# Diagonal masks on VectorE, and the weight sums and low parts made ahead on GpSimd's queue, in a hybrid decoder layer

## The chip, the cores and the metric

The kernel runs on one core of one Trainium2 chip. The metric is the device time of one execution in microseconds (us). An engine's instructions run in the order of its own queue; between engines only semaphores order the work. PE is TensorE, ACT is ScalarE, DVE is VectorE, POOL is GpSimd, SP is SyncE, which here only issues DMAs.

## The reference

One layer over 512 tokens of width 1024, batch 1:

```python
h = rms_norm(x, g_mix)
qa, ka, va, qb, kb, vb, gates = split(h @ w_in)            # 8 + 8 heads of 64
ya = moba_attention(rope(qa), rope(ka), va)                # causal softmax, blocks of 256
yb = stick_breaking_attention(qb, kb, vb)
#   z = q.k / 8; causal where s < t (strictly); log_1m = where(causal, -softplus(z), 0)
#   after = reverse exclusive cumsum(log_1m); a = where(causal, exp(log_sigmoid(z) + after), 0); y = a @ v
g = sigmoid(gates + b_gate)
x = x + (g[0] * (ya @ w_a) + g[1] * (yb @ w_b)) @ w_out
h = rms_norm(x, g_ffn)
u = causal_depthwise_conv(h @ w_up, conv_w, conv_b)        # width 3
x = x + (silu(u_gate) * u_val) @ w_down                    # d_ff 2816
out = rms_norm(x, g_final)
```

## The kernel before

All products are in float32 precision made of three fp32r matmuls: a weight block `raw` [128 x 1024] is loaded, ACT copies it to `whi` (the high part), DVE subtracts to get `wlo` (the low part), and `mm3` (L75) multiplies high by high, high by low, low by high: L76, L77, L78. `wload` (L59) does load and split; `raw` has five buffers, `whi`/`wlo` three, so the split of a weight waits until PE has finished the weight three places earlier.

The order of PE's instructions is the order in which the code is written. Of the other engines' instructions a scheduler sets the order from estimated times; where `issue_after` or the helper `inline` (L709) is used, the order on ACT and DVE is written out by hand.

The stages, with their times in the profile:

- 0 to 33 us: norm and the first projections. 33 to 131: attention a (two calls of `attend`, L426), with other projections as fillers between its steps (the lists GAPS).
- 131 to 222: attention b, the stick-breaking one, two calls of `attend` for two head pairs each. A call has three units of query tiles: unit 0 holds tiles 0 and 1, unit 1 tile 2, unit 2 tile 3. For each unit and pair, `weights_b` (L397) takes the scores from PSUM: ACT writes s1 = sigmoid(-z) and be = sigmoid(z), POOL masks the diagonal 128-column blocks of both for both heads (`affine_select`, L406: above the diagonal s1 becomes 1 and be 0), DVE runs a reversed product scan of s1 into R (L414) and multiplies be by it (L416). Then `turn` transposes the result on PE (L443, tile `tp`, one buffer) and ACT copies it out (L446, tile `aT`). s1 (named `a1`), be (`a2`) and R have two buffers each. The filler projections end in DVE instructions that empty a PSUM bank of `pmm` (two buffers): `o` (L338, L340) for q and k, `g` (L489) for the gates.
- 222 to about 340 us, the gates stage: the loop over `KT` (L567): gate projections (`g`), branch products with the weights `ab`, and `split_ahead` twice in an iteration.
- about 340 to 390: the out projection (weights `out`, sums `osum`), the residual x1 and its norm (`x1_add`, `x1_sq`, `x1_scale`), transposes (`x1_turn`) and their drains `x1_out`, which write the high and low rows `h` that the up projection multiplies. This passage is called the up seam.
- 390 to 610: the up projection with convolution and gate. Row tiles 4 to 15 (`MIXED`) are multiplied in a Winograd-like scheme of 7 products for 8 that needs sums of weight blocks, `usum`. 610 to 728: the down projection, final norm and output.

The sums: `sums_of` (L238) makes `usum` of one row tile by four DMAs on POOL's queue, DRAM to DRAM: a copy of 1024 KB, an accumulating add of 512 KB, two accumulating adds of 256 KB. Six tiles are made from 30 us on, with the four `osum` of the out projection; the other six are queued behind the last `affine_select` of attention b. `split_ahead` makes the low part of usum blocks 2 and 3 for nine of the tiles ahead of time: a load `praw` on SP's queue, the high part `phi` on ACT (L562), the difference on DVE (L564), a store to DRAM, `ulo`, on SP's queue. In the mixed stage `wmix` (L889) then loads `wlo` from `ulo` on POOL's queue (L896) for these tiles, and computes it on DVE (L899) for the other three.

Of the kernel before, what the change touches and what calls it, by code (L numbers as in the profile page):

```python
# [10 lines left out]
F32 = mybir.dt.float32  # L11
F32R = mybir.dt.float32r
BF = mybir.dt.bfloat16
AF = mybir.ActivationFunctionType
OP = mybir.AluOpType
# [11 lines left out]
NWARM = 9 * (448,) + (128,)  # L27
NP = FT // 2
MIXED = range(4, 16)
EARLY = 6  # L30
AHEAD = MIXED[:9]
NL = 3
WORDER = ([(n, k) for n in ("qk0", "va") for k in range(4)] + [("vb", g, h) for g in range(2) for h in range(2)]
          + [("mqk", n, i) for n in range(2) for i in range(2)] + [("sqk", p, n) for p in range(4) for n in range(2)]
# [8 lines left out]
def trunk_layer(ctx: ExitStack, tc: tile.TileContext, x: bass.AP, xT: bass.AP, w: bass.AP, vec: bass.AP,  # L43
                gfin: bass.AP, trig: bass.AP, out: bass.AP):
    nc = tc.nc

    def pool(stack, name, bufs, space=None, side=None):
        kw = {}
        if space is not None:
            kw["space"] = space  # L50
        if side is not None:
            kw["side"] = side
        return stack.enter_context(tc.tile_pool(name=name, bufs=bufs, reuse_waits="tile", **kw))

    ctx.enter_context(tc.manual_schedule(engines={mybir.EngineType.PE}))
    consts = pool(ctx, "consts", 1)
    wraw = pool(ctx, "wraw", 5)
    wsp = pool(ctx, "wsp", 3)
# [78 lines left out]
    xp = pool(st1, "xp", 6)  # L137
# [6 lines left out]
    for n in NWARM:  # L144
# [3 lines left out]
    nc.gpsimd.affine_select(out=mf, in_=mf, pattern=[[-1, 128]], compare_op=OP.is_ge, fill=NEG, base=0,  # L148
                            channel_multiplier=1)
    nc.vector.tensor_copy(maskb, mf)  # L150
    xks = {}

    def square(k):
# [65 lines left out]
    def flat(key, n):  # L219
        return w[WIDX[key]:WIDX[key] + n].rearrange("i p (h c) -> (i p h c)", h=2).rearrange("(n p c) -> n p c", p=128, c=512)  # L220

    def adds(out, in_):
        nc.gpsimd.dma_start(out, in_, accum_op=OP.add, max_dma_last_dim=8192)
# [3 lines left out]
    with tc.issue_after(nc.gpsimd.tensor_copy(small[:, 31:], r1[:, :1]).ins):  # L227
        for j, q in enumerate(osum):
            nc.gpsimd.dma_start(q, flat(("oi", j, 0), 2), max_dma_last_dim=8192)
        for j, q in enumerate(osum):  # L230
            adds(q[0:2], flat(("oi", j, 2), 1))
        for q in osum:
            adds(q[2], q[1])
        for q in osum:
            adds(q[3], q[2])
        usum = {i: wdr.tile([4, 128, 512], F32, name=f"usum{i}") for i in MIXED}

        def sums_of(pairs, n=3):  # L238
            for group in (pairs[j:j + n] for j in range(0, len(pairs), n)):
                for i in group:  # L240
                    nc.gpsimd.dma_start(usum[i], flat(("ui", i, 0), 2), max_dma_last_dim=8192)
                for i in group:
                    adds(usum[i][0:2], flat(("ui", i, 2), 1))
                for i in group:
                    adds(usum[i][3], usum[i][0])
                for i in group:
                    adds(usum[i][2], usum[i][3])

        sums_of(MIXED[:EARLY])

    mqkp = pool(ysta, "mqkp", 4, side="right")
    hlp = pool(ysta, "hlp", 2, side="right")
# [36 lines left out]
    def fill(n):  # L289
        while n > 0 and fillers:  # L290
            try:
                n -= next(fillers[0])
            except StopIteration:
                fillers.pop(0)
# [97 lines left out]
                nc.vector.tensor_scalar(a[:, h, o:o + n], a[:, h, o:o + n], st_[:, 1, i:i + 1], None, op0=OP.mult)  # L392
        return a

    selects = []

    def weights_b(sc, seg):  # L397
        W = seg[-1][1] + seg[-1][2]
        s1 = att.tile([128, 2, 512], F32, name="a1")
        nc.scalar.activation(s1[:, :, :W], sc[:, :, :W], AF.Sigmoid, scale=-1.0)  # L400
        be = att.tile([128, 2, 512], F32, name="a2")
        nc.scalar.activation(be[:, :, :W], sc[:, :, :W], AF.Sigmoid)
        for z, fill in ((s1, 1.0), (be, 0.0)):
            for qt, o, n in seg:
                zz = z[:, :, o + n - 128:o + n]
                selects.append(nc.gpsimd.affine_select(out=zz, in_=zz, pattern=[[0, 2], [-1, 128]],  # L406
                                                       compare_op=OP.is_ge, fill=fill, base=-1, channel_multiplier=1))
        R = att.tile([128, 2, 514], F32, name="R", bufs=2)
        for j, (qt, o, n) in enumerate(seg):
            r0 = o + j  # L410
            nc.vector.memset(R[:, :, r0 + n:r0 + n + 1], 1.0)
            for h in range(2):
                z = s1[:, h, o:o + n]
                nc.vector.tensor_tensor_scan(R[:, h, r0:r0 + n][:, ::-1], z[:, ::-1], z, 1.0,  # L414
                                             op0=OP.mult, op1=OP.bypass)
            nc.vector.tensor_mul(be[:, :, o:o + n], be[:, :, o:o + n], R[:, :, r0 + 1:r0 + n + 1])  # L416
        return be
# [90 lines left out]
    gsig = pool(ysta, "gsig", 6, side="right")  # L508
    attend("b", (0, 1), GAPS_B)
    attend("b", (2, 3), GAPS_B)  # L510
    with tc.issue_after(selects[-1].ins):
        sums_of(MIXED[EARLY:])
    fill(1000)
    psA.close()
    psB = ExitStack()
# [32 lines left out]
    psp = pool(tst, "psp", 1)  # L548
    ulo = {i: wdr.tile([128, 2, 512], F32R, name=f"ulo{i}") for i in AHEAD}
    ahead = list(AHEAD)  # L550

    def both(q):
        return q.rearrange("h p c -> p h c")

    def split_ahead():
        if not ahead:
            return
        i = ahead.pop(0)
        raw = psp.tile([128, 2, 512], F32, name="praw", bufs=2)
        nc.sync.dma_start(raw, both(usum[i][2:4]))  # L560
        hi = psp.tile([128, 2, 512], F32R, name="phi")
        nc.scalar.activation(hi, raw, AF.Copy)  # L562
        lo = raw.bitcast(F32R)
        nc.vector.tensor_sub(lo, raw, hi.bitcast(F32))  # L564
        nc.sync.dma_start(ulo[i].bitcast(F32), raw)

    for i in range(KT):  # L567
        if i >= NG:
# [32 lines left out]
    osp = pool(ost, "osp", 4, side="right")  # L601
# [92 lines left out]
    def x1_add(t, h):  # L694
        sl = slice(h * 512, (h + 1) * 512)
        op = nc.vector.tensor_sub if h else nc.vector.tensor_add
        ins = op(x1[:, t, sl], x1[:, t, sl], oq[f"c{t // 2 + 1}{h + 1}"][t % 2])
        nc.sync.dma_start(x1D[t][:, sl], x1[:, t, sl])
        return ins
# [4 lines left out]
    def x1_sq(t, h):  # L704
        return nc.scalar.activation(sqj, x1[:, t, h * 512:(h + 1) * 512], AF.Square, accum_out=sums2[:, h, t:t + 1])
# [3 lines left out]
    def inline(*steps):  # L709
        for f in steps:  # L710
            n = len(nc.cur_bb.bb.instructions)
            with ExitStack() as st:
                for i in tail.values():
                    st.enter_context(tc.issue_after(i))
                f()
            for i in nc.cur_bb.bb.instructions[n:]:
                if i.engine in (mybir.EngineType.DVE, mybir.EngineType.Activation):
                    tail[i.engine] = i

    def x1_scale(T):  # L720
        ts = slice(2 * T, 2 * T + 2)
        v, *rest = (small[:, 8 * T + 2 * i:8 * T + 2 * i + 2] for i in range(4))
        nc.vector.tensor_add(v, sums2[:, 0, ts], sums2[:, 1, ts])
        nc.vector.tensor_scalar(v, v, 1.0 / D, EPS, op0=OP.mult, op1=OP.add)
        r = rsqrt(v, *rest)
        for h in range(2):
            sl = slice(h * 512, (h + 1) * 512)
            for t in range(2):
                o, i, c = x1n[T][:, t, sl], x1[:, 2 * T + t, sl], r[:, t:t + 1]
                if t:  # L730
                    nc.scalar.activation(o, i, AF.Copy, scale=c)
                else:
                    nc.vector.tensor_scalar(o, i, c, None, op0=OP.mult)
# [9 lines left out]
    def x1_out(T, h, order=(0, 2, 1, 3)):  # L743
        for i in order:
            k = 4 * h + i
            src = turn_banks[T, h][i // 2][:, (i % 2) * 256:(i % 2 + 1) * 256]
            hl = h2[k][:, :, T * 256:(T + 1) * 256]
            act = nc.scalar.activation(hl[:, 0], src, AF.Copy, scale=gffn[:, k:k + 1])  # L748
            dve = nc.vector.scalar_tensor_tensor(hl[:, 1], src, gffn[:, k:k + 1], hl[:, 0].bitcast(F32),  # L749
                                                 op0=OP.mult, op1=OP.subtract)  # L750
# [4 lines left out]
    def upload_hi(p):  # L755
        raw = rload(("up",) + upq.pop(0))
        wup.append((p.tile([128, 1024], F32R, name="whi"), p.tile([128, 1024], F32R, name="wlo"), raw))
        nc.scalar.activation(wup[-1][0], raw, AF.Copy)

    def upload_lo(n):  # L760
        hi, lo, raw = wup[n]
        nc.vector.tensor_sub(lo, raw, hi.bitcast(F32))
# [14 lines left out]
           *(lambda t=t: x1_add(t, 1) for t in (2, 3)), lambda: upload_hi(wsp), lambda: upload_hi(wsp))  # L777
    inline(lambda: nc.scalar.activation(sqj[:, :1], padt[:, :1], AF.Sqrt), *(lambda t=t: x1_sq(t, 1) for t in (2, 3)))
    inline(*(lambda t=t, f=f: f(t, 0) for t in (2, 3) for f in (x1_add, x1_sq)), lambda: upload_lo(0))
    inline(lambda: x1_scale(1), lambda: upload_lo(1), *(lambda t=t, f=f: f(t, 0) for t in range(2) for f in (x1_add, x1_sq)))  # L780
    for t in range(2):
        for j, (xs, wa) in enumerate(second):
            mm3(oq["c12"][t], tuple(xs[:, c, 1, t * 128:(t + 1) * 128] for c in range(2)), blk(wa, 1, 512),
                False, j == HP - 1, skip_group_check=True)
            if t == 1 and j == 1:
                for h in range(2):
                    x1_turn(1, h)
    inline(lambda: x1_add(0, 1), lambda: x1_out(1, 0), lambda: x1_out(1, 1), lambda: x1_sq(0, 1), lambda: x1_add(1, 1),
           lambda: upload_hi(osp), lambda: x1_sq(1, 1), lambda: upload_lo(2), lambda: x1_scale(0), lambda: upload_hi(wsp))
    UPB = (6, 7, 4, 5, 0, 1, 2, 3)  # L790
    upn = [0]

# [367 lines left out]
```

## Time and profile before

| what | value |
|---|---|
| median of 3 runs | 727.8 us (727.79 to 728.9) |
| the profiled execution | 729.69 us, span 728.0 us |
| busy in the span: PE, DVE, ACT, POOL | 710.0, 560.7, 389.6, 85.9 us |
| granted TensorE clock, mean of the span | 0.990 |
| DMA share: SP's queue (q1), POOL's queue (q0) | 41.0%, 22.4% of 16 engines |

The span is the time from the first to the last instruction. Rows of the timeline begin with the start in us from the span's start and the duration in us; the bracket at a row's end is the time that the engine sat idle before it, and what ended that. Rows of waits give total us, times, longest us.

### The profile page before, as it was taken

The numbers are of one execution on the slowest core, as the hardware profiler recorded it, in microseconds if no ns is written. First come the engines' busy times: TensorE is split into PE (matmuls) and PEld (weight loads), VectorE is DVE, ScalarE is ACT, GpSimd is POOL, SyncE is SP. The second block draws the span as 40 slices with busy tenths as digits, with TensorE's granted clock in tenths as the row PEclk, the third lists the DMA queues.
The fourth block names the chain that finished last, engine by engine and source line by source line (L and its number), as shares of the span: only waits on it lengthen the run. The fifth ranks groups of instructions, "written<-read, shape, count | busy, mean of one in ns | idle before, by whom it ended". The sixth has DMA issues, their size and how long they took to land.

```text
span 728.0 us, 11232 instructions
## 1 busy us (share of the span) xinstructions
PE 710.0 (98%) x4316; PEld 612.7 (84%) x4316; DVE 560.7 (77%) x830; ACT 389.6 (54%) x582; POOL 85.9 (12%) x130
## 2 busy tenths in 40 slices
PE   9999999999999995999999999999999999999996
PEld 6888888889888884878879899999998888888884
DVE  7678867593973715577786898888999878988987
ACT  6335534563653304346375656766666445455764
POOL 0212333230432230000003300000000000000000
PEclk9999999999999997999999999999999999999998
DMA  8799999121149998757756937776655322567703
GB/s 313 265 341 327 249 235 243 57 88 59 62 141 362 255 259 302 268 199 251 271 173 211 225 93 240 233 259 209 212 184 164 113 91 87 171 197 249 266 13 117
DMA packets 45830, 146.60 MB, mean 201 GB/s; under 512 B 5072, under 2 KB 5840, under 8 KB 41680
## 3 DMA queue, kind: packets, MB, share of 16 engines
q1 hardware_dynamic: 37280, 103.08, 41.0%
q0 software_dynamic: 8208, 42.47, 22.4%
q8 instruction: 34, 0.56, 0.3%
q10 hardware_dynamic: 288, 0.33, 0.1%
q14 instruction: 20, 0.16, 0.1%
HBM read 132.75 MB, written 42.47 MB: 241 GB/s over the span
## 4 chain that ended last, share of the span: by engine, by line
PE 75%; DMA 12%; issue 4%; DVE 4%; ACT 3%; POOL 0%; SPq 0%; POOLq 0%; ACTq 0%; DVEq 0%
PE b L77 10%; PE b L78 10%; PE b L76 10%; PE mm L76 7%; PE mm L78 6%; PE mm L77 6%; DMA praw<-usum 5%; PE c L76 4%; PE c L78 4%; PE c L77 4%; PE q L188 3%; DMA usum<-w 3%; PE tp L443 2%; DMA usum<-usum 2%; PE tp L465 2%
## 5 line engine op out<-in xcount | busy, mean ns | idle before, releaser
L77 PE MATMUL b<-h,whi 128*128 128x256 f32 (+1 forms) x336 | 109.2, 325 | 0.2
L76 PE MATMUL b<-h,whi 128*128 128x256 f32 (+1 forms) x336 | 108.8, 324 | 0.5 <-ACT h L748 0.5
L78 PE MATMUL b<-h,wlo 128*128 128x256 f32 (+1 forms) x336 | 108.6, 323 | 0.0
L71 ACT ACTIVATE whi<-raw 128x1024 fp32r<-128x1024 f32 (+2 forms) x70 | 68.4, 985 | 72.2 <-PE b L77 22.5
L72 DVE TENSOR_TENSOR wlo<-raw,whi 128x1024 fp32r<-128x1024 f32 (+2 forms) x70 | 78.7, 1132 | 20.2 <-ACT whi L71 19.9
L76 PE MATMUL mm<-xg,whi 128*128 128x512 f32 x224 | 89.9, 401 | 0.0
L78 PE MATMUL mm<-xg,wlo 128*128 128x512 f32 x224 | 87.4, 390 | 0.0
L77 PE MATMUL mm<-xg,whi 128*128 128x512 f32 x224 | 87.3, 390 | 0.0
L76 PEld LDWEIGHTS b<-h,whi 128*128 128x128 f32 x336 | 63.9, 190 | 5.9 <-ACT h L748 0.9
L77 PEld LDWEIGHTS b<-h,whi 128*128 128x128 f32 x336 | 63.9, 190 | 5.8 <-DVE h L749 0.8
L78 PEld LDWEIGHTS b<-h,wlo 128*128 128x128 f32 x336 | 63.9, 190 | 4.9
L619 ACT ACTIVATE whi<-raw 128x1024 fp32r<-128x1024 f32 x45 | 46.8, 1051 | 35.4 <-DVE raw L637 16.2
L897 ACT ACTIVATE whi<-raw 128x1024 fp32r<-128x1024 f32 (+1 forms) x48 | 45.6, 951 | 34.6 <-PE b L77 28.9
L619 DVE TENSOR_TENSOR wlo<-raw,whi 128x1024 fp32r<-128x1024 f32 x45 | 54.7, 1221 | 7.4 <-ACT whi L619 7.2
L78 PE MATMUL b<-xa,wlo 128*128 128x256 f32 x192 | 54.5, 284 | 1.1 <-DMA wlo<-ulo 1.1
L76 PE MATMUL b<-xa,whi 128*128 128x256 f32 x192 | 54.3, 283 | 0.0
L77 PE MATMUL b<-xa,whi 128*128 128x256 f32 x192 | 54.3, 283 | 0.0
L76 PEld LDWEIGHTS mm<-xg,whi 128*128 128x128 f32 x224 | 42.1, 188 | 10.2 <-issue 1.8
L78 PEld LDWEIGHTS mm<-xg,wlo 128*128 128x128 f32 x224 | 42.1, 188 | 9.1
L77 PEld LDWEIGHTS mm<-xg,whi 128*128 128x128 f32 x224 | 42.2, 188 | 7.8
L899 DVE TENSOR_TENSOR wlo<-raw,whi 128x1024 fp32r<-128x1024 f32 (+1 forms) x39 | 41.3, 1058 | 9.4 <-ACT whi L897 8.9
L78 PEld LDWEIGHTS b<-xa,wlo 128*128 128x128 f32 x192 | 36.8, 192 | 1.5 <-DMA wlo<-ulo 1.5
(260 smaller groups left out, 1641.4 us busy)
## 6 DMA issues: line engine op xcount, KB each, us to landing
raw<-w SPq DMA_DIRECT2D x113, 512.0 KB, 4.2
usum<-w POOLq DMA_DIRECT2D x12, 1024.0 KB, 22.9
raw<-usum SPq DMA_DIRECT2D x24, 512.0 KB, 4.2
usum<-w POOLq DMA_DIRECT2D x12, 512.0 KB, 20.8
usum<-usum POOLq DMA_DIRECT2D x24, 256.0 KB, 11.1
raw<-w SPq DMA_DIRECT2D x22, 256.0 KB, 5.0
praw<-usum SPq DMA_DIRECT2D x9, 512.0 KB, 6.3
ulo<-praw SPq DMA_DIRECT2D x9, 512.0 KB, 3.8
```

The lines of the kernel that those rows point to most:

```text
L71: nc.scalar.activation(hi[:, sl], raw[:, sl], AF.Copy)
L72: nc.vector.tensor_sub(lo[:, sl], raw[:, sl], hi[:, sl].bitcast(F32))
L76: nc.tensor.matmul(ps, a[0], b[0], start=start, stop=False, **kw)
L77: nc.tensor.matmul(ps, a[0], b[1], start=False, stop=False, **kw)
L78: nc.tensor.matmul(ps, a[1], b[0], start=False, stop=stop, **kw)
L188: nc.tensor.matmul(qk0[c], w0[i][:, (k % 2) * 512 + c * 128:(k % 2) * 512 + (c + 1) * 128], xg[k][:, j], start=(k == 0 and n == 0), stop=( ...
L443: nc.tensor.transpose(tp[:, h, c:c + 128], a[:, h, c:c + 128], ident)
L465: nc.tensor.matmul(av[h * 64:(h + 1) * 64, j, qt * 128:(qt + 1) * 128], v[:, kb, (2 * p + h) * 64:(2 * p + h + 1) * 64], aT[p][:, h, o + k ...
L619: splits.append((nc.scalar.activation(hi, raw, AF.Copy), nc.vector.tensor_sub(lo, raw, hi.bitcast(F32))))
L897: nc.scalar.activation(hi[:, :n], raw[:, :n], AF.Copy)
L899: nc.vector.tensor_sub(wlo[:, :n], raw[:, :n], hi[:, :n].bitcast(F32))
```

## The change

Four edits:

1. `weights_b` masks with two [128 x 128] bf16 tables, `past` and `later`, made at the start on POOL: DVE takes max(s1, later) and be * past on each diagonal block. POOL has no part in attention any more.
2. All twelve `usum` tiles are queued at 30 us, in groups of three by the code. The scheduler hoists the copies: POOL's queue then holds 16 copies, 16 adds of 512 KB, and 32 adds of 256 KB, and no second group behind attention.
3. `split_ahead` covers all twelve tiles, and both its DMAs are on POOL's queue. The store writes the DVE result as fp32r, without a view as fp32.
4. In the up seam the squares of tiles 0 and 1 and one of the two last residual adds are put behind the eight drains `x1_out(1, .)`, and the third split of an up weight ahead of them.

```diff
-EARLY = 6
-AHEAD = MIXED[:9]
+AHEAD = MIXED
...
+    past, later = (consts.tile([128, 128], BF, name=n) for n in ("past", "later"))
+    for m, v in ((past, 0.0), (later, 1.0)):
+        mv = xp.tile([128, 128], F32, name="mv", bufs=2)
+        nc.gpsimd.memset(mv, 1.0 - v)
+        nc.gpsimd.affine_select(out=mv, in_=mv, pattern=[[-1, 128]], compare_op=OP.is_ge, fill=v, base=-1,
+                                channel_multiplier=1)
+        nc.gpsimd.tensor_copy(m, mv)
...
-        sums_of(MIXED[:EARLY])
+        sums_of(MIXED)
...
-        for z, fill in ((s1, 1.0), (be, 0.0)):
+        for z, m, op in ((s1, later, OP.max), (be, past, OP.mult)):
             for qt, o, n in seg:
                 zz = z[:, :, o + n - 128:o + n]
-                selects.append(nc.gpsimd.affine_select(out=zz, in_=zz, pattern=[[0, 2], [-1, 128]],
-                                                       compare_op=OP.is_ge, fill=fill, base=-1, channel_multiplier=1))
+                nc.vector.tensor_tensor(zz, zz, m[:, None].to_broadcast([128, 2, 128]), op=op)
...
-    with tc.issue_after(selects[-1].ins):
-        sums_of(MIXED[EARLY:])
...
-        nc.sync.dma_start(raw, both(usum[i][2:4]))
+        nc.gpsimd.dma_start(raw, both(usum[i][2:4]))
         hi = psp.tile([128, 2, 512], F32R, name="phi")
         nc.scalar.activation(hi, raw, AF.Copy)
         lo = raw.bitcast(F32R)
         nc.vector.tensor_sub(lo, raw, hi.bitcast(F32))
-        nc.sync.dma_start(ulo[i].bitcast(F32), raw)
+        nc.gpsimd.dma_start(ulo[i], lo)
...
-    inline(lambda: x1_scale(1), lambda: upload_lo(1), *(lambda t=t, f=f: f(t, 0) for t in range(2) for f in (x1_add, x1_sq)))
+    inline(lambda: x1_scale(1), lambda: upload_hi(osp), *(lambda t=t: x1_add(t, 0) for t in range(2)), lambda: upload_lo(1))
...
-    inline(lambda: x1_add(0, 1), lambda: x1_out(1, 0), lambda: x1_out(1, 1), lambda: x1_sq(0, 1), lambda: x1_add(1, 1),
-           lambda: upload_hi(osp), lambda: x1_sq(1, 1), lambda: upload_lo(2), lambda: x1_scale(0), lambda: upload_hi(wsp))
+    inline(lambda: x1_out(1, 0), lambda: x1_out(1, 1), lambda: x1_add(0, 1),
+           *(lambda t=t, h=h: x1_sq(t, h) for t, h in ((0, 0), (1, 0), (0, 1))), lambda: x1_add(1, 1), lambda: x1_sq(1, 1), lambda: upload_lo(2), lambda: x1_scale(0), lambda: upload_hi(wsp))
```

The order of PE's instructions is the same before and after. Line numbers in the rows of the change are those of the changed file, some lines off (whi is L70 there, phi L563, yb L474, g L493, scan L417, mul L419).

First place, the start of the gates stage. SP's queue before, behind the 30 weight loads that carry the kernel from 13 us to here:

```order
L560 DMA praw<-usum_399 128x2x512
L560 DMA praw<-usum_400 128x2x512
L66 DMA raw<-w 128x1024 x2
L565 DMA ulo_2598<-praw 128x1024
L66 DMA raw<-w 128x1024
L565 DMA ulo_2599<-praw 128x1024
```

ACT in the change, at the end of attention b (`g` is the gates' sigmoid; `yb` is the high part of the attention output; `whi` the split of a weight; before, the first `phi` stood behind both `yb`, a `whi` and a `g`):

```order
L493 ACTIVATE g<-g,vecs 128x512
L563 ACTIVATE phi<-praw 128x1024 x2
L474 ACTIVATE yb_1599<-tp 128x512
L474 ACTIVATE yb_1600<-tp 128x512
L70 ACTIVATE whi<-raw 128x1024
L563 ACTIVATE phi<-praw 128x1024
L493 ACTIVATE g<-g,vecs 128x512
L563 ACTIVATE phi<-praw 128x1024
L70 ACTIVATE whi<-raw 128x1024 x2
L563 ACTIVATE phi<-praw 128x1024 x2
```

SP's queue holds no praw and no ulo in the change, only weight loads; ACT's first two phi have moved ahead of yb, and the twelve phi go on between the next ten whi.

Second place, DVE in the first call of attention b, unit 0 and the beginning of unit 1. Before:

```order
L416 TENSOR_TENSOR a_1598<-a_1598,R 128x2x256
L414 SCALAR_TENSOR_TENSOR R<-a_1617 128x128 x2
L414 SCALAR_TENSOR_TENSOR R<-a_1617 128x256 x2
L286 TENSOR_SCALAR vb<-mm,n1r 128x256
L411 MEMSET R 128x2
L416 TENSOR_TENSOR a_1619<-a_1619,R 128x2x128
L72 TENSOR_TENSOR wlo<-raw,whi 128x1024
```

and in the change (a_1632 and a_1649 are the s1 of the two pairs, a_1634 and a_1651 their be):

```order
L410 TENSOR_TENSOR a_1632<-a_1632,later 128x2x128 x2
L475 TENSOR_TENSOR ya_88<-tp,ya_88 128x512
L417 SCALAR_TENSOR_TENSOR R<-a_1632 128x128 x2
L417 SCALAR_TENSOR_TENSOR R<-a_1632 128x256 x2
L410 TENSOR_TENSOR a_1634<-a_1634,past 128x2x128 x2
L410 TENSOR_TENSOR a_1649<-a_1649,later 128x2x128 x2
L410 TENSOR_TENSOR a_1651<-a_1651,past 128x2x128 x2
L419 TENSOR_TENSOR a_1634<-a_1634,R 128x2x128
L292 TENSOR_SCALAR vb<-mm,n1r 128x256
L419 TENSOR_TENSOR a_1634<-a_1634,R 128x2x256
L417 SCALAR_TENSOR_TENSOR R<-a_1649 128x128 x2
L71 TENSOR_TENSOR wlo<-raw,whi 128x1024
```

Eight masks stand in DVE's row in unit 0, ahead of the second pair's scans, and a `wlo` has moved in between those scans.

Third place, ACT in the up seam (`oa` is the scaled x1, `h` the drains, `ot,sums` the squares). Before:

```order
L731 ACTIVATE oa_3565<-x_3354,small 128x512 x2
L705 ACTIVATE ot_3563,sums_3562<-x_3354 128x512 x2
L748 ACTIVATE h_3333<-b_3326,vecs 128x256
L748 ACTIVATE h_3335<-b_3327,vecs 128x256
L748 ACTIVATE h_3334<-b_3326,vecs 128x256
```

and in the change:

```order
L732 ACTIVATE oa_3566<-x_3355,small 128x512 x2
L759 ACTIVATE whi<-raw 128x1024
L749 ACTIVATE h_3334<-b_3327,vecs 128x256
L749 ACTIVATE h_3336<-b_3328,vecs 128x256
L749 ACTIVATE h_3335<-b_3327,vecs 128x256
```

One weight split stands where the two squares stood; all four squares of tiles 0 and 1 are behind the eight drains.

More of the change, by code (lines that the diff above doesn't have):

```diff
@@ L393, in weights_a @@
         return a
-    selects = []
     def weights_b(sc, seg):
```

## The prediction

> **What bounds the kernel now.** I read the page's busy times first, then PE's waits, then PE's timeline where a wait stands, and only then the engines behind it.
>
> ```profile
> span 728.0 us, 11232 instructions
> PE 710.0 (98%) x4316; PEld 612.7 (84%) x4316; DVE 560.7 (77%) x830; ACT 389.6 (54%) x582; POOL 85.9 (12%) x130
> ```
>
> PE is busy for all but 18 us of the span, and its work does not change. So a gain can only come from its few waits, and a loss from new ones. PE's waits:
>
> ```profile
> PE mm L76 <- ACT whi L71: 5.9, 1, 5.9
> PE mm L78 <- DVE wlo L72: 1.9, 2, 1.6
> ...
> PE b L78 <- DMA wlo<-ulo: 1.1, 2, 0.6
> ```
>
> One wait is large: 5.9 us for a weight's high part, in the gates stage. PE's timeline there, and the stretch as a whole (PE busy, PEld, DVE, ACT, POOL, then granted clock, DMA share, GB/s):
>
> ```profile
> 263.50 0.39 PE L76 MATMUL mm<-xg,whi 128*128 128x512 f32 x1
> ...
> 274.15 0.39 PE L78 MATMUL mm<-xg,wlo 128*128 128x512 f32 x1
> 280.40 0.80 PE L76 MATMUL mm<-ya,whi 128*128 128x512 f32 x1 [5.86 <-ACT whi L71]
> ...
> 287.00 0.40 PE L78 MATMUL mm<-ya,wlo 128*128 128x512 f32 x1
> ```
>
> ```profile
> 275.00:287.00 12.00, 5.05 (x12) 3.52 (x13) 7.44 (x10) 5.10 (x6) 0.00 (x0) 0.57 0.89 333
> ```
>
> From 263.50 to 274.15 stand 47 steps: 0.227 us a matmul. From 274.15 to 287.00 stand 12, which at that pace are 2.72 us and took 12.85. So the stall costs 10.1 us, more than the listed waits of 5.9 and 1.6, because the granted clock falls to 0.57 behind it. Who is to blame stands on SP, ACT and POOL:
>
> ```profile
> 257.41 0.38 SPq L560 DMA_DIRECT2D praw<-usum  x1
> ```
> ```profile
> 278.34 1.06 ACT L562 ACTIVATE phi<-praw 128x1024 fp32r<-128x1024 f32 x1 [18.59 <-DMA praw<-usum]
> 279.31 1.04 ACT L71 ACTIVATE whi<-raw 128x1024 fp32r<-128x1024 f32 x1
> ```
> ```profile
> 212.55 3.15 POOL L241 DMA_DIRECT2D usum<-w  x6
> ...
> 269.01 0.77 POOL L223 DMA_DIRECT2D usum<-usum  x1 [0.73 <-DMA usum<-usum]
> ```
>
> The sums of the last six tiles are issued from 212.55 to 269.01. In that time a praw issued at 257.41 is not there until 278.3, `phi` holds ACT for 18.6 us, and the `whi` that PE needs stands behind it. The DMA answers for 215 to 275 us (first row) and 285 to 330 (the others) show how much is contention, KB each and median us to landing:
>
> ```profile
> praw<-usum SPq DMA_DIRECT2D x4, 512.0 KB, 18.6
> ```
> ```profile
> praw<-usum SPq DMA_DIRECT2D x5, 512.0 KB, 5.0
> ulo<-praw SPq DMA_DIRECT2D x5, 512.0 KB, 3.0
> ```
>
> **Term 1, sums and low parts: -10.1 us.** The whole stall goes if two things hold.
>
> First, all sums must have landed before attention b ends. In POOL's queue before, with ten copies, ten adds and twenty small adds, an issue waits for the DMA eight places earlier:
>
> ```profile
> 41.67 0.52 POOL L241 DMA_DIRECT2D usum<-w  x1 [2.54 <-issue]
> ...
> 76.47 1.08 POOL L223 DMA_DIRECT2D usum<-w  x1 [2.17 <-issue]
> ...
> 103.50 0.87 POOL L223 DMA_DIRECT2D usum<-usum  x1 [1.85 <-DMA usum<-w]
> ...
> 120.82 0.77 POOL L223 DMA_DIRECT2D usum<-usum  x1 [1.01 <-DMA osum<-osum]
> ```
>
> Nine copies landed from 41.67 to 76.47 (3.87 us each), ten adds up to 103.50 (2.70), twelve small adds up to 120.82 (1.44). The eight left end at about 132. Six more tiles take 6 x (3.87 + 2.70 + 2 x 1.44) = 57 us, so the last lands near 189. The weight loads of attention b then share the DMA engines until 189, as those of attention a did, where PE had no wait.
>
> Second, the twelve rounds praw, phi, difference, ulo must keep up on POOL's queue. Praw waits until DVE has last used R, whose memory it takes. The last product with R moves by the five us of term 2, to about 218.5:
>
> ```profile
> 212.56 1.22 DVE L416 TENSOR_TENSOR a<-a,R 128x1024 f32<-128x1024 f32 x1 [1.05 <-POOL a L406]
> ```
> ```profile
> 230.86 0.39 PE L76 MATMUL mm<-ya,whi 128*128 128x512 f32 x1
> ```
>
> So the first phi can run at 218.5 + 5.0 = 223.5, and the two are over long before yb is due: PE multiplies yb first 12 matmuls after 230.86, at 233.6. With two buffers, a pair of rounds takes 5.0 (praw) + 1.1 (phi) + 1.2 (DVE) + 3.0 (ulo) + 0.8 and 0.8 (two more issues at 0.77) = 11.9 us, and the eleventh phi comes five pairs later, at 283. Ten `whi` stand between the first two phi and the last: the one behind the eleventh phi is for the weight eleven places after the one that begins at 230.86. At 24 x 0.227 = 5.44 us a weight PE reaches it at 290.7, with term 2 at 292.8; less 1.1 and 1.2 for high and low part, that phi has until 290. There are 6 to 7 us in hand, or a pair time of up to 13.2. I take the full 10.1. The three more phi (1.06) and differences (1.2) lie on ACT and DVE, which are idle for most of this stage.
>
> **Term 2, masks on DVE: +2.1 us (0.3 to 4.5).** A mask is a tensor_tensor of 256 columns. The nearest rows are the product by R and what surrounds it:
>
> ```profile
> 138.26 0.60 DVE L414 TENSOR_TENSOR_SCAN R<-a 128x128 f32<-128x128 f32 x1 [1.91 <-POOL a L406]
> ...
> 144.89 0.41 DVE L416 TENSOR_TENSOR a<-a,R 128x256 f32<-128x256 f32 x1
> ...
> 145.23 1.21 DVE L72 TENSOR_TENSOR wlo<-raw,whi 128x1024 fp32r<-128x1024 f32 x1
> ...
> 162.38 0.66 DVE L338 SCALAR_TENSOR_TENSOR o<-mm,rb 128x512 f32<-128x512 f32 x1
> ...
> 208.58 1.20 DVE L416 TENSOR_TENSOR a<-a,R 128x1024 f32<-128x1024 f32 x1
> ```
>
> It is 0.41 us by itself and 0.34 start to start. I take 0.36, since some masks are followed by an instruction that reads their result. There are 32: 11.5 us more for DVE, of which only that counts which makes PE late. [...]
>
> Three places on PE's path:
>
> ```profile
> 144.70 0.81 ACT L400 ACTIVATE a<-sc 128x768 f32<-128x768 f32 x1 [0.70 <-DVE R L414]
> ...
> 148.06 0.81 ACT L446 ACTIVATE aT<-tp 128x768 f32<-128x768 f32 x1
> ```
> ```profile
> 150.60 0.60 PE L443 MATMUL tp<-ident,a 128*128 128x128 f32 x4
> ...
> 166.06 0.28 PE L76 MATMUL mm<-whi,xg 128*128 128x256 f32 x1
> ...
> 166.41 0.28 PE L76 MATMUL mm<-whi,xg 128*128 128x256 f32 x1
> ...
> 213.46 0.71 PE L443 MATMUL tp<-ident,a 128*128 128x128 f32 x5
> ```
>
> - First call, unit 0. The second pair's scans, ended by 144.5, are now behind eight masks, a vb and a wlo. Two masks fill the wait of 1.91; the rest is 0.3 + 6 x 0.36 + 0.4 + 1.1 = 4.0, so they end at 148.5. ACT's sigmoid of unit 1 (144.70) waits for them, since it takes their buffer, and behind it in ACT's queue come a whi, the other sigmoid and aT: 3.2 us, aT done near 151.6. PE writes the same tp tile at 150.60. Lost: 1.0.
> - First call, unit 2. The `o` at 162.38 frees the PSUM bank that PE takes at 166.06. Fifteen masks are ahead of it: 0.3 + 13 x 0.36 = 5.0, so it ends at 167.3 to 168.0, against 167.1 for PE with the first loss. Lost: 0.6.
> - Second call, unit 2. The product at 208.58 ends at 209.8; the same 5.0, less 1.2 of waits for POOL that go, makes 213.6, against PE's 213.46. Lost: 0.1 to 0.5, and some for smaller places: 0.5.
>
> The low end is a mask of 0.34 with nothing lost in the second call; the high end one of 0.41 with 0.1 for each dependence.
>
> **Term 3, up seam: -1.7 us (-0.3 to -1.8).**
>
> ```profile
> 378.19 0.63 ACT L705 ACTIVATE ot<-x 128x512 f32<-128x512 f32 x1 [1.36 <-issue]
> ...
> 379.58 0.82 ACT L748 ACTIVATE h<-b,vecs 128x256 fp32r<-128x256 f32 x2
> ```
> ```profile
> 379.20 0.40 PE L78 MATMUL b<-whi,xs 128*128 128x512 f32 x1
> 380.09 0.38 PE L76 MATMUL b<-h,whi 128*128 128x256 f32 x1 [0.49 <-ACT h L748]
> ```
> ```profile
> 380.00:390.00 10.00, 9.74 (x73) 9.13 (x74) 7.27 (x19) 7.53 (x17) 0.00 (x0) 1.00 0.53 189
> ```
>
> The drains wait behind two squares that themselves waited 1.36. PE lost 0.66 at 380.09 (0.89 against a step of 0.23), and then 72 matmuls of 256 columns, 0.12 each by the rows at 166.06 and 166.41 (three steps), fill the stretch from 380 to 390, where 8.6 us would do: 1.2 to 1.3 more. With a weight split of 1.0 in place of wait and squares, the drains start at about 377.9, 1.7 earlier, and stay ahead of PE. The moved squares come after the drains; the second half's transposes need them, three half passes of PE (8.6 us) later, which covers eight drains and four squares of 0.63. The low end is what is left if DVE's half of the drains becomes the limit.
>
> **Term 4, reads of ulo: +0.4 us (0 to 1.7).** Two of nine `wlo<-ulo` made PE wait about 0.55 (1.1 in the list above). Three more such reads at the same rate cost 3 x 2/9 x 0.55; if all three are late, 1.7. The three differences that DVE is spared there had room. POOL's two tables are made at the start, where POOL then waits until 30 us anyway: nothing.
>
> Sum: -10.1 + 2.1 - 1.7 + 0.4 = -9.3 us. The profiled execution took 729.69, which is 1.9 above the median of 727.8; I apply the sum to the median: 718.5 us.
>
> **Rivals.**
> - The stall moves to POOL's queue. If a pair takes 14.5 us instead of 11.9 (three DMAs of 512 KB per weight share the engines, and POOL issues in strict order, so one late difference holds the next load), the eleventh phi comes 5 x 2.6 = 13 us later, 6.5 more than there is in hand, and PE waits for that: about 725. For it: 6.5 us in hand is little. Against: 5.0 and 3.0 were measured with the same mix. 0.16.
> - The sums land late, so that the change does not do what it says: `phi` now stands ahead of `yb` on ACT. It costs nothing up to 225 us; with the first praw at 235, two phi and both halves of yb end at 239, 3 us after PE wants it at 233.6 + 2.1: 722. It would take 46 us on top of 189. 0.04.
> - Slower than before: DVE becomes the bound in attention b, because masks and scans form one chain there and every mask is exposed. 32 x 0.41 = 13.1 in place of 2.1 gives 729.5. It turns slower than before once more than (9.3 + 2.1) / 32 = 0.36 us of each mask is exposed. Against: the product that ends at 209.8 is used at 213.46, and the `o` that ends at 163.0 at 166.06; 3 us and more are in hand before the first mask shows. 0.05.
> - [...] 0.03.
>
> **How the numbers follow.** The forecast has 0.72. Its own ends are 727.8 - 10.1 + 0.3 - 1.8 = 716.2 and 727.8 - 10.1 + 4.5 - 0.3 + 1.7 = 723.6; the range reaches a little past both, 715.5 to 724.5, which takes in the second rival and most of the first. A measurement of this kernel tells 0.2% (1.5 us) from no change. Faster: the forecast, the first two rivals nearly whole: 0.91. Same: 0.03. Slower: what the last two rivals leave: 0.06.
>
> **What would show it.** Term 1: no PE wait for whi or wlo between 222 and 330 us, granted clock 1.00 there, the last usum issue near 180, praw landing in 5 to 6 us. Term 2: PE waits at L443 for ACT's aT and at a first matmul for `o` or `g`, 1 to 4 us in all, none before. Term 3: no wait for h L748, the first drain right behind a weight split. Term 4: waits for wlo<-ulo, 1 to 2.5 us. I am wrong if ACT still waits over 6 us at a phi, or if PE's waits in attention b add up to more than 5 us.

## The result, and the profile after

The changed kernel takes 720.51 us (median of 4 runs, 719.39 to 722.6) against 727.86 (4 runs, 727.79 to 728.9): a ratio of 0.990 [0.987, 0.993]. The forecast was 718.5, with a range of 715.5 to 724.5. The profiled execution took 722.6 us, its span is 7.4 us shorter than before. Its page:

```profile
span 720.6 us, 11212 instructions
PE 705.9 (98%) x4316; PEld 611.2 (85%) x4316; DVE 568.7 (79%) x862; ACT 392.5 (54%) x585; POOL 81.8 (11%) x131
```

PE's waits after (total us, times, longest us):

```profile
PE b L77 <- DMA wlo<-ulo: 4.7, 3, 2.7
PE tp L446 <- ACT aT L449: 1.7, 1, 1.7
PE mm L144 <- DVE warmb L138: 1.3, 1, 1.3
```

The waits for whi, wlo and h are gone. In their place stand a wait in attention b (L446) and longer waits for reads of ulo. When the same matmul is looked up in both timelines, its lead over before shows where each part arose: 0.65 us by 28 us, nothing more up to 208, then 1.94 lost at one place in attention b, 10.8 won in the gates stage (10.2 by 300 us, 0.6 between there and 330), 1.45 in the up seam, 3.8 lost at reads of ulo, and 0.2 won at 613. That makes 7.4.

**Gates stage.** The stretch that held the stall (PE, PEld, DVE, ACT, POOL busy, granted clock, DMA share, GB/s), and the DMA answer for 222 to 330 us:

```profile
275.00:287.00 12.00, 12.00 (x54) 9.96 (x53) 7.65 (x10) 6.11 (x7) 2.55 (x4) 1.00 0.67 220
```
```profile
ulo<-praw POOLq DMA_DIRECT2D x12, 512.0 KB, 3.3
praw<-usum POOLq DMA_DIRECT2D x10, 512.0 KB, 4.9
```

PE is busy for 12.00 of the 12.00 us where it was for 5.05, the clock is 1.00 where it was 0.57, and praw lands in 4.9 us where it took 18.6. POOL's timeline gives the reason, the last sum and the first praw, and ACT's the first, the ninth and the eleventh phi:

```profile
176.10 0.77 POOL L229 DMA_DIRECT2D usum<-usum  x1 [1.00 <-DMA usum<-usum]
216.22 1.51 POOL L561 DMA_DIRECT2D praw<-usum  x2 [39.35 <-DVE g L492]
```
```profile
223.58 1.05 ACT L563 ACTIVATE phi<-praw 128x1024 fp32r<-128x1024 f32 x1
...
272.79 1.06 ACT L563 ACTIVATE phi<-praw 128x1024 fp32r<-128x1024 f32 x1 [6.95 <-DMA praw<-usum]
...
284.70 1.06 ACT L563 ACTIVATE phi<-praw 128x1024 fp32r<-128x1024 f32 x1 [4.22 <-DMA praw<-usum]
```

The last sum, issued at 176.10, lands 10.9 us later, so that none is in flight any more when the first praw is issued at 216.22. The first phi runs at 223.58 and the eleventh at 284.70: five pairs of 12.2 us.

**Attention b, second call.** PE, DVE and ACT around the one new wait:

```profile
207.35 0.82 PE L446 MATMUL tp<-ident,a 128*128 128x128 f32 x6
...
210.42 1.22 DVE L419 TENSOR_TENSOR a<-a,R 128x1024 f32<-128x1024 f32 x1
...
211.56 0.68 DVE L492 TENSOR_TENSOR g<-mm,rb 128x512 f32<-128x512 f32 x1
...
212.28 0.72 ACT L493 ACTIVATE g<-g,vecs 128x512 f32<-128x512 f32 x1 [4.26 <-DVE g L492]
...
213.81 0.80 ACT L449 ACTIVATE aT<-tp 128x768 f32<-128x768 f32 x1
...
214.66 1.09 PE L446 MATMUL tp<-ident,a 128*128 128x128 f32 x8 [1.69 <-ACT aT L449]
```

The product that the transposes at 214.66 read is there at 211.64, before they are due (214.66 - 1.69 = 212.97). What is late is the tile tp: its last contents, transposed from 207.35, have stood there since 208.17, but ACT copies them out only at 213.81. ACT's queue holds a sigmoid of the gates ahead of that copy, and the sigmoid waits 4.26 us for DVE's `g`, which stands behind masks, scans and the product. Before, ACT's order was the same:

```profile
209.69 0.68 DVE L489 TENSOR_TENSOR g<-mm,rb 128x512 f32<-128x512 f32 x1
...
210.41 0.73 ACT L490 ACTIVATE g<-g,vecs 128x512 f32<-128x512 f32 x1 [2.08 <-DVE g L489]
...
211.94 0.80 ACT L446 ACTIVATE aT<-tp 128x768 f32<-128x768 f32 x1
```

There aT ended at 212.74, 0.7 us before PE's transposes at 213.46. So the loss takes both: DVE's `g` came 2.5 us later against PE's positions (1.9 by the rows, and the 0.65 from the start), and ACT's order handed that on to aT.

**Attention b, first call.** ACT in unit 0, where the prediction put a loss of 1.0:

```profile
146.68 0.81 ACT L404 ACTIVATE a<-sc 128x768 f32<-128x768 f32 x1 [3.43 <-DVE R L414]
...
149.03 0.82 ACT L449 ACTIVATE aT<-tp 128x768 f32<-128x768 f32 x1
```

aT ends at 149.85, and PE's next transposes begin at 149.90, with no wait in PE's list.

**Up seam.** ACT's split of the third up weight, its first drains, and PE's first matmul with h:

```profile
367.24 1.04 ACT L759 ACTIVATE whi<-raw 128x1024 fp32r<-128x1024 f32 x1
368.19 0.81 ACT L749 ACTIVATE h<-b,vecs 128x256 fp32r<-128x256 f32 x2
...
369.94 0.28 PE L75 MATMUL b<-h,whi 128*128 128x256 f32 x1
```

The drains start right behind the split, before PE's transposes end, and PE finds h ready.

**Reads of ulo.** PE's three waits, and the last two issues on POOL's queue with what SP issues in between:

```profile
490.17 0.39 PE L77 MATMUL b<-xa,wlo 128*128 128x256 f32 x1 [0.87 <-DMA wlo<-ulo]
...
511.67 0.39 PE L77 MATMUL b<-xa,wlo 128*128 128x256 f32 x1 [1.08 <-DMA wlo<-ulo]
...
539.11 0.38 PE L77 MATMUL b<-xa,wlo 128*128 128x256 f32 x1 [2.71 <-DMA wlo<-ulo]
```
```profile
526.49 0.53 POOL L897 DMA_DIRECT2D wlo<-ulo  x1 [9.55 <-DVE u L929]
527.09 11.71 SPq L65 DMA_DIRECT2D raw<-w  x6
...
532.25 0.53 POOL L897 DMA_DIRECT2D wlo<-ulo  x1 [5.23 <-PE b L77]
```

The reads come every 10.1 us or so, but the last one only 5.8 us after the one ahead of it. It is issued at 532.25, when PE gives its buffer back, and PE wants it at 539.11 - 2.71 = 536.40. The other two late ones were issued 5.6 us before PE wanted them, at 483.67 and 505.00.

### The profile page after: what moved, and what is told of

It reads as the page before. It is cut to its first block, busy times and chain, and to the rows that moved or that the text cites. A ratio compares the mean times of both kernels' runs of the same rounds, so it can differ in the third digit from the quotient of the medians.

```text
span 720.6 us, 11212 instructions
## 1 busy us (share of the span) xinstructions
PE 705.9 (98%) x4316; PEld 611.2 (85%) x4316; DVE 568.7 (79%) x862; ACT 392.5 (54%) x585; POOL 81.8 (11%) x131
## 4 chain that ended last, share of the span: by engine, by line
PE 88%; DVE 5%; DMA 3%; issue 3%; ACT 2%; POOLq 0%; DVEq 0%; ACTq 0%
PE b L77 11%; PE b L76 11%; PE b L75 11%; PE mm L75 10%; PE mm L77 9%; PE mm L76 9%; PE c L75 4%; PE c L77 4%; PE c L76 4%; PE q L194 3%; DMA wlo<-ulo 3%; PE tp L468 3%; PE tp L446 2%; DVE R L417 1%; PE sc L370 1%
## 5 line engine op out<-in xcount | busy, mean ns | idle before, releaser
L70 ACT ACTIVATE whi<-raw 128x1024 fp32r<-128x1024 f32 (+2 forms) x70 | 68.6, 986 | 72.9 <-PE b L76 28.3
L900 DVE TENSOR_TENSOR wlo<-raw,whi 128x1024 fp32r<-128x1024 f32 (+1 forms) x36 | 37.6, 1045 | 11.1 <-ACT whi L898 10.7
```

Of the source, the lines that this page charges most:

```text
L70: nc.scalar.activation(hi[:, sl], raw[:, sl], AF.Copy)
L900: nc.vector.tensor_sub(wlo[:, :n], raw[:, :n], hi[:, :n].bitcast(F32))
```

## The experiments

Each time stands beside runs of the kernel before that were made with it on the same chip, as a ratio to those. PE's positions are compared with the timeline of the changed kernel, as above.

### What made the stall: the sums, or the queue of praw and ulo?

**Masks back on POOL** (edit 1 undone alone):

```diff
-        for z, m, op in ((s1, later, OP.max), (be, past, OP.mult)):
+        for z, fill in ((s1, 1.0), (be, 0.0)):
...
-                nc.vector.tensor_tensor(zz, zz, m[:, None].to_broadcast([128, 2, 128]), op=op)
+                selects.append(nc.gpsimd.affine_select(out=zz, in_=zz, pattern=[[0, 2], [-1, 128]],
+                                                       compare_op=OP.is_ge, fill=fill, base=-1, channel_multiplier=1))
```

> The changed kernel with only the masks back on POOL: its queue then holds all sums, up to the last issue at 176 us, ahead of the first mask. Theory (POOL works its queue in strict order, and its issues wait for earlier DMAs): the first mask, wanted at about 138, runs at 177; attention b stands for 30 to 38 us: about 755. Rival (the queue of DMAs holds up only DMAs): 718.5 to 720, since the masks cost DVE nothing.

Measured: 758.7 us, ratio 1.042 [1.040, 1.045]. PE's longest wait, POOL's last sum and first masks, and DVE's first scan:

```profile
PE mm L75 <- DVE R L417: 34.4, 1, 34.4
```
```profile
170.58 0.77 POOL L229 DMA_DIRECT2D usum<-usum  x1 [0.41 <-DMA usum<-usum]
171.09 4.52 POOL L412 TENSOR_SCALAR_AFFINE_SELECT a<-a 128x256 f32<-128x256 f32 x8
```
```profile
171.81 0.68 DVE L420 TENSOR_TENSOR_SCAN R<-a 128x128 f32<-128x128 f32 x1 [36.41 <-POOL a L412]
```

The first masks run as soon as the last sum is issued, and DVE's scan waits 36.41 us for them. So with all sums queued at 30 us the masks had to leave POOL: edits 1 and 2 are one change. (Sums queued in portions between the masks were not tried.)

**Masks alone**: the kernel before, with edit 1 only.

```diff
-    with tc.issue_after(selects[-1].ins):
+    with tc.issue_after(nc.gpsimd.tensor_copy(small[:, 30:31], selects[-1][:, 0, :1]).ins):
         sums_of(MIXED[EARLY:])
```

> The kernel before with only the masks moved to DVE; the six late sums stand behind a small copy on POOL that waits for the last product of attention b, 3 us later than before. Theory (the masks by themselves cost what the second call showed, and the late sums make the stall): 2.0 more in attention b, and a stall of 10 us or more near 280 us: 729 to 733. Rival (masks on DVE shorten the way, POOL's hops were the cost): 726 to 727.

Measured: 732.49 us, ratio 1.007 [1.006, 1.008]. PE's waits and the DMA answer for 215 to 275 us:

```profile
PE mm L76 <- ACT whi L71: 8.4, 1, 8.4
PE tp L450 <- ACT aT L453: 1.7, 1, 1.7
```
```profile
praw<-usum SPq DMA_DIRECT2D x4, 512.0 KB, 19.6
```

The same 1.7 at the same tile tp, and a stall that has grown from 5.9 to 8.4 with sums that end later. By itself edit 1 loses.

**praw and ulo on SP's queue** (that part of edit 3 undone alone):

```diff
-        nc.gpsimd.dma_start(raw, both(usum[i][2:4]))
+        nc.sync.dma_start(raw, both(usum[i][2:4]))
...
-        nc.gpsimd.dma_start(ulo[i], lo)
+        nc.sync.dma_start(ulo[i].bitcast(F32), raw)
```

> All sums still made early, but the loads praw and the stores ulo on SP's queue, as before the change. Theory (the stall came from the sums that were still in flight at 212 to 270 us): praw lands in 5 us, no wait for whi in the gates stage, 720.5 within 1. Rival (the queue is what counts: on SP the loads and stores stand among the weight loads and hold them up in strict order): PE waits for whi or wlo in the gates stage, 3 to 10 us more, 723 to 730.

Measured: 723.25 us (12 runs, 719.04 to 726.37), ratio 0.994 [0.992, 0.996]. By the time alone the rival would have won. The profile says otherwise; the DMA answer for 222 to 330 us, PE's longest wait, and a stretch behind that wait:

```profile
praw<-usum SPq DMA_DIRECT2D x10, 512.0 KB, 4.2
```
```profile
PE b L77 <- DMA wlo<-ulo: 3.4, 1, 3.4
```
```profile
538.00:548.00 10.00, 9.95 (x53) 9.23 (x54) 6.33 (x10) 3.02 (x4) 0.00 (x0) 0.83 0.31 113
```

There is no wait in the gates stage: PE is 0.50 us behind the changed kernel's positions at 219 us and 0.50 at 360, which it was from the start. This execution lost its time at the last read of ulo, 3.42 us, and some 1.5 more because the granted clock fell to 0.83 behind it. So the early sums alone take the stall away, and which queue issues praw and ulo does not matter for it. (This span is only 0.5 us longer than the profiled one of the changed kernel, which was its longest execution. What makes the medians 2.7 us apart in the others, no trace shows.) The queue was tried again once the reads of ulo made PE wait no more (the kernel with own buffer and moved filler, below): the same edit in that kernel,

> The same kernel with the loads praw and the stores ulo on SP's queue. Theory (early sums alone take the stall away; what the run with praw and ulo on SP lost was a late read of ulo near 538 us, which the own buffer covers): 716.7 within 0.5. Rival (the queue counts, the weight loads behind praw come later in some executions): 718 to 720.

took 716.01 us (715.5 to 717.36), ratio 0.983 [0.981, 0.985], beside 716.7 and 0.985 [0.983, 0.987] without it. From 28 us to the end PE's positions in the two profiles stay 0.2 us apart, so no gain of the queue can be told.

### Why the reads of ulo come late

**Eleven tiles ahead**: the last tile's low part on DVE.

```diff
-AHEAD = MIXED
+AHEAD = MIXED[:11]
```

> The last of the mixed tiles gets its low part on DVE again, the other eleven read it back. Theory (the last read has too little lead): no first half of a next tile stands between its buffer's release and its use, so it is issued 4.0 us before PE needs it, against 5.6 for the others, and takes 6.7 to land; without it PE's wait of 2.7 at 539 us goes, the two waits of 0.9 and 1.1 stay: about 717.8 us against 720.5. Rival (the DMA engines are full there and whatever is loaded is late): the weight that PE waits for is another one, the time stays at 720.5 within 0.5. Rival (reads from POOL's queue have become slow as a class): waits stay spread over the other reads, less than 1 us is won.

Measured: 719.2 us, ratio 0.990 [0.988, 0.992]. PE's waits for reads:

```profile
PE b L77 <- DMA wlo<-ulo: 1.4, 1, 1.4
```

The wait at 539 is gone, and against the changed kernel PE gains 3.0 us there; the read that was late at 511 came in time here, the one at 490 later (1.40 for 0.87). So these waits differ between executions. In five profiles with twelve reads (the changed kernel, the runs with praw on SP and with the masks on POOL, and the runs with the filler moved and with the old seam below) they add up to 4.7, 3.4, 4.2, 3.3 and 0.9; the last read was late in four of the five, by 2.71, 3.42, 3.48 and 2.35. What does not differ is the place. In every profile so far, before included, PE waited only for the seventh, the ninth or the twelfth read, never for another one. The time is no proof here: 1.3 us less than 720.51, with runs from 717.43 to 720.95.

**Own buffer**: the last weight of a mixed tile uses 512 columns only, and its low part gets a buffer of that size.

```diff
-        wlo = wsp.tile([128, 1024], F32R, name="wlo")
+        wlo = wsp.tile([128, 1024], F32R, name="wlo") if n == 1024 else wdl.tile([128, n], F32R, name="wdl")
...
     prev = None
+    wdl = pool(hst, "wdl", 1)
```

> Of the four weights of a mixed tile the last uses 512 columns only; its low part gets a buffer of its own of that size, so that the three buffers of wlo are shared by three weights of a tile and not by four. A read of ulo then has 7.2 us from its issue to PE's need of it (three weights of 2.9, 2.9 and 1.45), the last one too, against 5.6 and 4.0. Theory (the reads are late for want of lead, 3.5 to 6.8 us to landing): no wait for wlo<-ulo is left; the four profiles with twelve reads lost 4.7, 3.3, 0.9 and 3.4 there, so some 3.1 less than 720.5: about 717.4. Rival (the DMA engines are full in that stage, and something is always late): PE waits for another weight instead, 720.5 within 0.7.

Measured: 717.95 us (717.52 to 718.56), ratio 0.987 [0.985, 0.988]. All of PE's waits:

```profile
PE tp L446 <- ACT aT L449: 1.7, 1, 1.7
PE mm L144 <- DVE warmb L138: 1.3, 1, 1.3
```

No wait for a read is listed any more, although the reads now take 4.7 us to land (median) against 4.0. The last one only just came in time: it took 7.0 us, and PE's matmul at 533.91 stands 0.2 us behind its pace. Nothing was made faster; they were asked for earlier. That settles it against the rival of full DMA engines, by which PE would have waited for another weight. Why just those reads take longer to land was not tried: the median of the twelve is 4.0 us in the changed kernel, and the last one took 6.8.

### The order in attention b

**Filler moved**: one filler step of the second call from ahead of the second transposes of unit 1 to behind them. In ACT's queue only the gates' sigmoid moves, behind aT.

```diff
-    attend("b", (2, 3), GAPS_B)
+    attend("b", (2, 3), (8, 4, 5, 4, 3, 4, 8, 5, 5))
```

> In the second call of attention b one filler step moves from before the second transposes of unit 1 to after them. The only thing that moves in ACT's queue is one sigmoid of the gates, which now stands behind the copy aT instead of ahead of it. Theory (PE's wait of 1.7 at 214.66 is ACT's order: aT stands behind a sigmoid that waits 4.3 us for DVE): the wait goes, 1.7 to 1.9 us less, about 718.7. Rival (DVE's chain of masks, scans and products is itself late there): PE waits for the product instead, 720.5 within 0.5.

Measured: 721.43 us (719.02 to 724.27), ratio 0.993 [0.990, 0.995]: by time no gain can be told. In the profile the wait for aT is down to 0.3, and PE has gained 1.4 us from 190 to 219; it waits 3.3 at reads of ulo. So it was run again on top of the own buffer:

> The own buffer for the last low part and the moved filler step of attention b together. Theory (two separate waits): 3.1 and 1.7 less, about 715.7. Rival (one of the two is given back later): about 717.5.

Measured: 716.7 us (716.37 to 717.26), ratio 0.985 [0.983, 0.987], beside 717.95 for the own buffer alone: 1.25 less by the medians, and 1.7 by the spans, 715.7 and 714.0. ACT's queue there, and PE's waits:

```profile
209.09 0.80 ACT L449 ACTIVATE aT<-tp 128x768 f32<-128x768 f32 x1
212.40 0.73 ACT L493 ACTIVATE g<-g,vecs 128x512 f32<-128x512 f32 x1 [2.51 <-DVE g L492]
```
```profile
PE mm L144 <- DVE warmb L138: 1.3, 1, 1.3
PE tp L446 <- ACT aT L449: 0.3, 1, 0.3
```

aT runs 4.7 us earlier. The masks, the scans and `g` on DVE are as late as they were (`g` at 211.68, 211.56 in the changed kernel); only what stood behind them on ACT was moved, with one step of PE's filler. So what edit 1 costs, it costs through ACT's order behind DVE's later `g`, and 1.4 of the 1.94 us are to be had back without making DVE faster.

### The up seam, and the three additional tiles

**Seam in its old order** (edit 4 undone alone, in the changed kernel and then in the kernel with own buffer and moved filler):

```diff
-    inline(lambda: x1_out(1, 0), lambda: x1_out(1, 1), lambda: x1_add(0, 1),
...
+    inline(lambda: x1_add(0, 1), lambda: x1_out(1, 0), lambda: x1_out(1, 1), lambda: x1_sq(0, 1), lambda: x1_add(1, 1),
...
```

> The up seam alone in its old order. Theory (the drains behind the squares cost what the sum took): PE waits for h again, 1.5 to 1.7 us more, 722.1. Rival (what was gained there is lost later to the next wait, so the edit is worth nothing by itself): 720.5 within 0.5.

Measured: 720.49 us, ratio 0.992 [0.989, 0.994], the time of the changed kernel. PE's waits:

```profile
PE b L77 <- DMA wlo<-ulo: 0.9, 1, 0.9
PE b L75 <- ACT h L749: 0.5, 1, 0.5
```

The wait for h is back, and PE's positions show 1.45 us lost between 360 and 376 and 0.2 more at 613. This execution happened to lose 0.9 at the reads where the changed kernel's lost 4.7. With the reads out of the way:

> The kernel with the own buffer and the moved filler step (716.7 us), with the up seam in its old order. Its reads of ulo make PE wait no more, so the size of the seam can be told by time. Theory (the seam's edit is worth the 1.8 that PE's positions showed): 718.5. Rival (it is given back before the end): 716.7 within 0.5.

Measured: 717.94 us (717.22 to 718.36), ratio 0.986 [0.984, 0.987]. By time the size stays open. The same kernel with the seam changed took 716.7, 1.2 less, but on another chip, and its ratio of 0.985 is no different; the two kernels run beside this one, 1.9 and 2.4 us shorter, differ from it in one thing more. PE's positions tell: against the profile of the kernel with the seam changed, 1.46 us are lost in the seam and 0.2 at 607, and nothing is given back before the end. So the seam is worth 1.65 us, and the rival falls.

**Nine tiles ahead**, as before the change, in the same kernel (`AHEAD = MIXED[:9]`):

> The same kernel with nine tiles' low parts made ahead, as before the change; DVE splits the last three weights of the mixed stage again. Theory (three differences of 1.2 on DVE have room, and the reads no longer cost anything): 716.7 within 0.5. Rival (DVE is late in the mixed stage, where it is busy for 136 of 154 us): PE waits for wlo from DVE, 1 to 3 us more.

Measured: 715.49 us (715.28 to 716.18), ratio 0.983 [0.981, 0.984], the lowest median, though not clear of 716.01. PE has no wait for DVE's three differences, and from 28 us to the end its positions stay 0.4 us ahead of the profile with twelve tiles. So neither part of edit 3, the three more tiles or the other queue, brings a gain that can be told, and in the changed kernel as it stands the twelfth read costs PE 2.7 us. The gain of the change is the early sums, which the masks on DVE make possible, and the seam.

## Why the prediction was right, and where it was not

The time was in the range, 2.0 us above the forecast.

- **Term 1 (-10.1).** 10.8 by PE's positions, 10.2 of it where the stall stood.
  - The other 0.6 is not shown to come from the early sums: it is a wait of 0.32 for DVE's wlo at 318 us with what followed it, and the run with the masks alone, whose sums were late, did not have it either.
  - The two conditions held: the last sum was issued at 176.10 and landed at 187.0 (near 180 and 189 were forecast), the eleventh phi ran at 284.70 (283, with a limit of 290), a pair took 12.2 us (11.9). That the first phi ran at 223.58, where 223.5 was forecast, is luck: its praw was issued 2.3 us earlier than assumed and landed 4.0 us later, at 220.25, and phi then stood behind aT, a whi and a sigmoid in ACT's queue. DVE was not idle for most of this stage, as the prediction says (66 of the 118 us from 222 to 340 before), but the added differences made nothing late.
  - One of the signs named there was set too sharply: ACT does wait 6.95 us at a phi, at 272.79. PE lost nothing by it, since the 6 us in hand covered it. It is PE's wait, not ACT's, that tells.
- **Term 2 (+2.1, 0.3 to 4.5).** 1.94 measured, and 1.93 with the masks alone. That the size fits is luck, since the places were wrong and two errors cancel. The first call, from which 1.0 and 0.6 were to come, lost nothing, and the second call, put at 0.5, lost all of it.
  - What the masks add to DVE's row was put too high. Against PE's positions the scans of unit 0 ended 2.6 us later and the `o` of unit 2 2.9, where 4.0 and 5.0 were forecast. In unit 0 ACT did wait for DVE as the prediction says, 3.43 us, but aT was done in time.
  - One thing that the sum left out: DVE's own work beside POOL's masks had been slower. Before, scans of 256 columns took 0.79 us on average where an `affine_select` ran at the same time and 0.66 where none did, products of 512 columns 0.89 and 0.68; with the masks back on POOL it is 0.82 and 0.66, 0.88 and 0.67; in the changed kernel 0.67 and 0.68.
  - In the second call the step that failed looked at DVE's product alone (late by 0.1 to 0.5 us). The product was in time by 1.3; what was late was ACT's aT, in strict order behind a sigmoid that waits for DVE. The prediction had that mechanism, but for the first call only.
- **Term 3 (-1.7).** 1.45 by positions in the seam and 0.2 at 613, and the same when undone, in both kernels (the 1.8 named in the expectation of the second of these runs is more than they show).
- **Term 4 (+0.4, 0 to 1.7).** 3.8 measured in the profiled execution, outside the term's bounds: this is the mis-sized term. Its 3.4 too little, less 0.7 from term 1 and 0.65 from the start, are what the time came out above the forecast; that it stayed in the range owes something to these two. The step was "three more such reads at the same rate". Lateness has no rate here: the tenth and the eleventh read, two of the three new ones, never made PE wait, and the twelfth is not such a read: it belongs to the last mixed tile, behind which no next tile's first two weights (5.8 us of PE) stand. It has 4.1 us from issue to use where the others have 5.6, and a landing of 6.8 then costs 2.7. With nine tiles ahead that read did not exist. Even the upper bound, three reads late by 0.55 each, took its price from reads with more lead.
- **Start.** 0.65 us were won by 28 us, which no term had. In the ten other kernels made from the changed one PE stood there from 0.3 us earlier to 0.9 later than in its profile. So it differs between executions by more than its size, and is not shown to be of the change.
- **Rivals.** The stall did not move to POOL's queue: 12.2 us a pair, not 14.5. The sums were not late. DVE did not become the bound: one place of 1.94 us, not 13.1. The issues of praw and ulo on POOL's queue were short, 0.55 to 0.77 us each, with a DVE instruction running beside all but two of the 24. On SP's queue praw landed in 4.2 us for 4.9, with no difference in time that could be told.

## What to carry to other kernels

When a stall is blamed on a wait, ask what was in flight there and whether it could have been done while the engines behind it were idle: here the early sums alone did it, and no gain could be told of the queue that was changed along with them. Price a prefetch by its lead, issue to use, of each single read, and look at the last one of a stage by itself, since nothing that comes next stands in front of it. And a cost put on one engine (masks on DVE) shows where another engine's strict order stands behind it; here a change of that order gave 1.4 of 1.94 us back.

## What the runs showed of the hardware

Of four waits of PE the two shorter ones left the granted clock at 1.00, and behind the two longer ones it was lower. The same read of ulo made PE wait 2.35, 2.71, 3.42 and 3.48 us in four profiles (the last with the masks on POOL). Behind 2.71, and behind 3.48, PE, PEld, DVE, ACT, POOL busy, granted clock, DMA share and GB/s:

```profile
539.00:549.00 10.00, 9.89 (x60) 8.90 (x61) 7.78 (x12) 3.80 (x6) 0.00 (x0) 1.00 0.50 154
```
```profile
573.00:583.00 10.00, 10.00 (x50) 9.39 (x51) 5.62 (x9) 3.02 (x4) 0.00 (x0) 0.73 0.27 96
```
```profile
573.32 0.42 PE L75 MATMUL b<-xa,whi 128*128 128x256 f32 x1
573.54 0.41 PE L76 MATMUL b<-xa,whi 128*128 128x256 f32 x1
573.75 0.41 PE L77 MATMUL b<-xa,wlo 128*128 128x256 f32 x1
```

Behind 2.35 and 2.71 the clock stays at 1.00; behind 3.42 it is 0.83 over ten us (shown above), behind 3.48 it is 0.73, with 0.21 us from one matmul to the next in place of 0.12, which cost some 1.5 and 2.4 us beyond the waits (the next 50 matmuls against the same ones in the profile with the own buffer). So in these profiles the waits that were 0.71 and 0.77 us longer than 2.71 cost 2.2 and 3.2 us more in all (0.71 + 1.5 and 0.77 + 2.4). From which length on a wait costs more than itself, four waits do not show. Such a cost would widen the spread of times, though no trace of the longest runs was kept to show it: the runs of the changed kernels with late reads lie 3.2 to 7.3 us apart, those without them 0.9 to 1.9.
